# Two decoder layers on one core: projections in column pairs by seven products, attention on plain fp32, and every engine in a planned order

## The chip, the cores and the metric

The kernel runs on one core of a Trainium2 chip. The core has five engines: TensorE (PE: matmuls and transposes, results in eight PSUM banks of 512 columns), VectorE (DVE), ScalarE (ACT), GpSimd (POOL) and SyncE (SP), whose queue issues all DMAs here. Each engine runs its own instructions in order and waits for the others by semaphores. The metric is the device time of one execution in microseconds; less is better.

## The reference

Two layers on x (1024 rows by 1024 columns), all in fp32:

```python
for l in range(DEPTH):                                   # 2
    ada = c_act @ w_ada[l] + b_ada[l]
    shift, scale, gate = jnp.split(ada, 3, axis=-1)
    h = rmsnorm(x, norm_g[l]) * (1.0 + scale[:, None, :]) + shift[:, None, :]
    p = h @ w_in[l]                                      # 1024 x 9224
    mq, mk, mv, mo, mz, mi, mf, rq, rk, rv, rz = split_cols(p)
    qk = jax.nn.silu(causal_dwconv(jnp.concatenate([mq, mk], axis=-1), conv_w[l], conv_b[l]))
    ...
    cell = mlstm_chunkwise(mq_c, mk_c, mv, mi + b_igate[l], mf + b_fgate[l])     # 4 heads x 256
    y_m = jax.nn.sigmoid(mo) * head_layernorm(cell, gn_m[l], N_HEADS_MLSTM) * jax.nn.silu(mz)
    ret = retention_chunkwise(rq_h, rk_h, rv)                                    # 4 heads x 256, rotary q, k
    y_r = head_layernorm(ret, gn_r[l], N_HEADS_RET) * jax.nn.silu(rz)
    y = jnp.concatenate([y_m, y_r], axis=-1) @ w_out[l]  # 2048 x 1024
    x = x + gate[:, None, :] * y
return rmsnorm(x, final_g)
```

Each head is causal and works chunk by chunk: scores of q and k under a mask of decays, times v, plus q times a state of 256 x 256 that each chunk updates (mLSTM has a further column for the normaliser), then a norm over the head's 256 columns.

## The kernel before, in words

**Number format.** TensorE takes its fast fp32r form of each operand, so every fp32 tile is split in two: a rounded part hi and the rest lo. `split_to` (L620) casts hi on ACT (L621) and subtracts on GpSimd or VectorE to get lo (L622). A product is `mm3` (L144 to L147): hi by hi, hi by lo, lo by hi.

**Projections.** The normalised x is kept transposed (`hT`, eight k tiles of 128 rows, two halves of 512 positions, hi and lo). A block is 128 columns of `w_in`: two loads of 256 KB (`load_w_raw`, L338), two splits into wH and wL, and `proj_units` (L363) with 8 k x 2 halves x 3 matmuls of 512 columns into a PSUM bank (`pp`). v is projected the other way round, positions on partitions, in `v_path` (L579): 8 row tiles x 8 k x 3 matmuls of 256 columns, so that its result has the layout that attention wants. Per layer there are 72 blocks and 8 gate columns: at first z and o of head 0 and a second z block (made k by k while the norm comes in, in layer 0 by a script string with the steps S, Q, N, K, T, H, F ... written out by hand, L1200 to L1281), then v of head 0 with the gate columns, then head after head: 0 to 3 mLSTM (q and k with a convolution over four positions, `qk_ml` with `conv_silu`, L630 to L644; v, z, o), 4 to 7 retention (q and k with rotary, `qk_ret`, L701 to L717; v, z).

**Attention.** `attention` (L743) works in four chunks of 256 rows, launched as a generator whose pieces run between pieces of the projections. Operands are split: scores from q and k in hi and lo (L145 to L147, and `diagonal`), state updates by L772 and `mm3`, values from the state (cH, cL, L855) and from the scores (sH, sL, L845 and `mm3`). q, k in columns and v come directly from the projections' PSUM banks. k is also needed by rows: it is transposed in blocks of 32 on VectorE, stored to a DRAM tile `kdr` (L653) and gathered back (L663, four DMAs a chunk with runs of 64 elements). Normalised results go out to `ndr` (L919), gates to `gdr` (L553); the output projection loads both, multiplies them (L972, L976), splits the product, and makes `out_units` (L985).

**Order.** TensorE's order is the one written by hand: what `run_units`, `launch` and `tick` (L120 to L142) emit. The other engines are ordered by the framework's scheduler. At the start a few matmuls on a constant (step D of the script, L1263) keep TensorE busy ahead of the first products. The sums of w_ada times silu(c), which give scale and shift, run on VectorE (L246, L266) and are summed over partitions by TensorE (L251).

Of the kernel before, what the change touches and what calls it, by code (L numbers as in the profile page):

```python
# [19 lines left out]
P = 128  # L20
# [58 lines left out]

@with_exitstack  # L80
def tile_hybrid_trunk(ctx, tc, x, xt, c, positions, w_ada, b_ada, norm_g, w_in, conv_w, conv_b,
                      b_igate, b_fgate, gn_m, gn_r, w_out, final_g, consts, out):
    nc = tc.nc
    V, A, G, PE, Q = nc.vector, nc.scalar, nc.gpsimd, nc.tensor, nc.sync

# [4 lines left out]
    big = ctx.enter_context(tc.tile_pool(name="big", bufs=62))  # L90
    wrk = ctx.enter_context(tc.tile_pool(name="wrk", bufs=2))
    dpool = ctx.enter_context(tc.tile_pool(name="dram", bufs=1, space=DRAM))
    pp = ctx.enter_context(tc.tile_pool(name="pp", bufs=4, space=PSUM))
    pa = ctx.enter_context(tc.tile_pool(name="pa", bufs=4, space=PSUM))
# [3 lines left out]
    def nm(s):  # L98
        uid[0] += 1
        return f"{s}_{uid[0]}"  # L100

    def bt(dt=F32, n=512):
        return big.tile([P, n], dt, tag="b", name=nm("b"))

    def wt(tag, n, bufs, dt=F32):
        return wrk.tile([P, n], dt, tag=tag, bufs=bufs, name=nm(tag))

    def ps_a():
        return pa.tile([P, 512], F32, tag="a", name=nm("pa"))

    def ps_p():
        return pp.tile([P, 512], F32, tag="p", name=nm("pp"))

    def f(ap):
        return ap.bitcast(F32)

    clock = [0]
    pending = []

    def launch(gen, delay=0):  # L120
        uid[0] += 1
        pending.append([clock[0] + delay, uid[0], gen])

    def tick():
        clock[0] += 1
        while True:
            due = [p for p in pending if p[0] <= clock[0]]
            if not due:
                return
            p = min(due, key=lambda q: (q[0], q[1]))  # L130
            try:
                p[0] = clock[0] + next(p[2])
            except StopIteration:
                pending.remove(p)

    def drain():
        while pending:
            tick()

    def run_units(gen):  # L140
        for _ in gen:
            tick()  # L142

    def mm3(o, lt, rt, start, stop):  # L144
        PE.matmul(o, lt[0], rt[0], start=start, stop=False)  # L145
        PE.matmul(o, lt[0], rt[1], start=False, stop=False)  # L146
        PE.matmul(o, lt[1], rt[0], start=False, stop=stop)  # L147

    ident = cst.tile([P, P], F32, tag="ident", name="ident")
    make_identity(nc, ident)  # L150
    ones = cst.tile([P, 1], F32, tag="ones", name="ones")
    V.memset(ones, 1.0)
    mhalf = cst.tile([P, 4], F32, tag="mhalf", name="mhalf")
    V.memset(mhalf, -0.5)
    rmask = cst.tile([P, 384], F32, tag="rmask", name="rmask")
    V.memset(rmask, 1.0)
    ones_r = cst.tile([P, P], F32R, tag="ones_r", name="ones_r")
    V.tensor_copy(ones_r, rmask[:, 0:P])
    G.affine_select(rmask[:, 0:256], rmask[:, 0:256], [[1, 256]], ALU.is_ge, 0.0, base=0, channel_multiplier=-1)
    G.affine_select(rmask[:, 256:384], rmask[:, 256:384], [[1, 128]], ALU.is_ge, 0.0, base=0, channel_multiplier=-1)  # L160
    kc = cst.tile([P, N_CONST], F32, tag="kc", name="kc")
    Q.dma_start(kc, consts)

    xdr = [dpool.tile([D, HALF], F32, name=f"xdr{i}") for i in range(2)]
    ndr = [[[dpool.tile([8, 32, HALF], F32, name=f"ndr{l}_{h}_{i}") for i in range(2)] for h in range(8)]
           for l in range(DEPTH)]
    gdr = [[[[dpool.tile([P, HALF], F32, name=f"gdr{l}_{h}_{m}_{i}") for i in range(2)] for m in range(2)]
            for h in range(8)] for l in range(DEPTH)]
    kdr = [[[dpool.tile([HD, HALF], F32, name=f"kdr{l}_{h}_{i}") for i in range(2)] for h in range(8)]
           for l in range(DEPTH)]  # L170
    mdr = [dpool.tile([NH, T], F32, name=f"mdr{l}") for l in range(DEPTH)]

    cols = [None, None]
    gsh = [cst.tile([P, 2, KT], F32, tag=f"gsh{l}", name=f"gsh{l}") for l in range(DEPTH)]

    def load_ada_rows(l):
        rows = wt("rows", P, 2)
        Q.dma_start(rows[0:8, :], norm_g[l].rearrange("(r c) -> r c", c=P))
        Q.dma_start(rows[8:32, :], b_ada[l].rearrange("(r c) -> r c", c=P))
        return rows  # L180

    def load_head_rows(l):
        rows = wt("rows", P, 2)
# [4 lines left out]
        bg = cst.tile([P, 1], F32, tag=f"bg{l}", name=f"bg{l}")  # L188
        Q.dma_start(bg[0:4, :], b_fgate[l].unsqueeze(1))
        Q.dma_start(bg[32:36, :], b_igate[l].unsqueeze(1))  # L190
        return rows, bg

    def ada_cols(l, rows):
        cl = cst.tile([P, P], F32, tag=f"cols{l}", name=f"cols{l}")
        bg = None
        pt = ps_a()
        PE.transpose(pt[:, 0:32], rows[0:32, :], ident[0:32, 0:32])
        V.tensor_copy(cl[:, 0:8], pt[:, 0:8])
        V.tensor_copy(cl[:, 104:128], pt[:, 8:32])
        cols[l] = (cl, bg)  # L200

    def head_cols(l, rb):
        rows, bg = rb
        cl = cols[l][0]
        pt = ps_a()
        PE.transpose(pt[:, 0:96], rows[0:96, :], ident[0:96, 0:96])
        V.tensor_copy(cl[:, 8:88], pt[:, 0:80])
        V.tensor_scalar(cl[:, 88:96], pt[:, 80:88], 0.25, None, ALU.mult)
        V.tensor_scalar(cl[:, 96:104], pt[:, 88:96], 0.5, None, ALU.mult)
        cols[l] = (cl, bg)  # L210

    def gn_col(l, h, ct):
        return cols[l][0][:, 88 + 2 * h + ct:89 + 2 * h + ct]

    cact = cst.tile([P, KT], F32, tag="cact", name="cact")
    cth = cst.tile([P, KT], F32, tag="cth", name="cth")

    def load_cact(crow):
        pt = ps_a()
        PE.transpose(pt[:, 0:8], crow[0:8, :], ident[0:8, 0:8])  # L220
        A.activation(cth, pt[:, 0:8], AF.Tanh, scale=0.5)
        V.scalar_tensor_tensor(cact, cth, 1.0, pt[:, 0:8], ALU.add, ALU.mult)
        V.tensor_scalar(cact, cact, 0.5, None, ALU.mult)

    def finish_gsh(l, k, n, psh, psc):
        cl = cols[l][0]
        V.tensor_tensor(gsh[l][:, 1, k:k + n], psh, cl[:, 104 + k:104 + k + n], ALU.add)
        t1 = wt("sm1", 4, 2)[:, 0:n]
        V.scalar_tensor_tensor(t1, psc, 1.0, cl[:, 112 + k:112 + k + n], ALU.add, ALU.add)
        V.tensor_tensor(gsh[l][:, 0, k:k + n], t1, cl[:, k:k + n], ALU.mult)  # L230

    def ada_load(l, g):
        raws = []
        for kk in range(KT):
            raw = bt()
            Q.dma_start(raw.rearrange("p (w c) -> p w c", w=2),
                        w_ada[l, kk * P:(kk + 1) * P].rearrange("p (w c) -> p w c", c=D)[:, 0:2, g * 256:(g + 1) * 256])
            raws.append(raw)
        return raws

    def ada_group(raws, acc, kks):
        for kk in kks:
            if kk == 0:
                V.tensor_scalar(acc, raws[0], cact[:, 0:1], None, ALU.mult)
            else:
                V.scalar_tensor_tensor(acc, raws[kk], cact[:, kk:kk + 1], acc, ALU.mult, ALU.add)  # L246

    def ada_sums(l, g, acc, pt):
        for which in range(2):
            for i in range(2):  # L250
                PE.matmul(pt[:, 4 * g + 2 * which + i:4 * g + 2 * which + i + 1],  # L251
                          acc[:, which * 256 + i * P:which * 256 + (i + 1) * P], ones, start=True, stop=True)

    def ada_rows(l, c0, accs):
        acc = bt()
        accs.append(acc)
        prev = None
        for k in range(KT + 1):
            raw = None
            if k < KT:  # L260
                raw = wt("raw", 512, 4)
                Q.dma_start(raw, w_ada[l, k * P:(k + 1) * P, c0:c0 + 512])
            if k == 1:
                V.tensor_scalar(acc, prev, cact[:, 0:1], None, ALU.mult)
            elif k > 1:
                V.scalar_tensor_tensor(acc, prev, cact[:, k - 1:k], acc, ALU.mult, ALU.add)  # L266
            prev = raw
            yield 2

    def ada_columns_later(l):  # L270
        for half in range(2):
            accs = []
            for which in range(2):
                yield from ada_rows(l, which * D + half * 512, accs)
            yield 2
            pt = ps_a()
            for which in range(2):
                for i in range(4):
                    PE.matmul(pt[:, which * 4 + i:which * 4 + i + 1], accs[which][:, i * P:(i + 1) * P], ones,
                              start=True, stop=True)  # L280
# [1122 lines left out]
```

## Time and profile before

| What | Before |
|---|---|
| time of the runs, median of 3 | 2299.13 us (2298.86 to 2301.01) |
| span of the profiled execution | 2298.7 us |
| instructions | 34322 |
| TensorE busy | 2269.4 us, 99% |
| VectorE busy | 1338.7 us, 58% |
| ScalarE busy | 926.5 us, 40% |
| GpSimd busy | 827.5 us, 36% |
| SP's DMA queue | 359932 packets, 257.00 MB, 39.8% of 16 DMA engines' span |
| mean granted TensorE clock | 0.999 |

How to read it: a busy time is the sum over an engine's instructions, each from its start to its end, overlaps counted once. Rows of the profile name line, engine, operation, out<-in tiles and shapes, then a count; "busy, mean ns" and the idle time just ahead of them, with what ended it, stand at the end. A timeline row has start and length in front and "xN" for N like instructions in a row. PE's ends are modelled (the page's mean of a 512-column matmul is 395 ns), so the distance between two starts tells more than a length. The profiled execution's time is its span; what lies around the span is not recorded, and the span is 0.4 us below the median of the runs.

### The profile page before, as it was taken

To read this page: it belongs to the slowest core of one execution; us is meant where nothing else is said; L and a number is where in the kernel's file an instruction comes from. 1 tells how busy PE (TensorE), PEld (TensorE's weight loads), DVE (VectorE), ACT (ScalarE), POOL (GpSimd) and SP (SyncE) were. 2 spreads that over 40 slices of the span, in tenths; PEclk is the share of its full clock that TensorE was granted. 3 is DMA by queue.
4 is the path that set the end of the run, shared out by engine and by line. 5 is a ranking of instruction groups with operands and counts; after the bars stand their busy time and mean duration, and the time that the engine had idled before them with its cause. 6 is when DMAs were issued, how large, how long until landed. Compare 5 with 4: busy or idle time off the path is not lost. (4 is left out here: it accounts for less than half of the span.)

```text
span 2298.7 us, 34322 instructions
## 1 busy us (share of the span) xinstructions
PE 2269.4 (99%) x12411; PEld 1953.7 (85%) x12411; DVE 1338.7 (58%) x2821; ACT 926.5 (40%) x1785; POOL 827.5 (36%) x820
## 2 busy tenths in 40 slices
PE   7999999999999999999999999999999999999998
PEld 5888888889988888988888889888898898988886
DVE  7467688556555555585435676555564545556563
ACT  7535433444332323343544454444343323234442
POOL 0343333333333334224562434333334334341313
PEclk9999999999999999999999999999999999999999
DMA  8333333324433533476532323233223233436674
GB/s 258 80 69 94 83 80 82 83 70 115 124 110 87 149 96 79 126 254 212 169 105 67 84 71 82 77 77 79 68 71 98 74 91 88 124 84 205 184 242 125
DMA packets 360246, 259.45 MB, mean 113 GB/s; under 512 B 113266, under 2 KB 297338, under 8 KB 360076
## 3 DMA queue, kind: packets, MB, share of 16 engines
q1 hardware_dynamic: 359932, 257.00, 39.8%
q8 instruction: 97, 1.59, 0.3%
q14 instruction: 73, 0.60, 0.1%
q10 hardware_dynamic: 144, 0.26, 0.0%
HBM read 201.57 MB, written 55.61 MB: 112 GB/s over the span
## 5 line engine op out<-in xcount | busy, mean ns | idle before, releaser
L145 PE MATMUL pp<-b,wH 128*128 128x512 f32 x1824 | 719.6, 395 | 0.0
L146 PE MATMUL pp<-b,wH 128*128 128x512 f32 x1824 | 718.6, 394 | 0.0
L147 PE MATMUL pp<-b,wL 128*128 128x512 f32 x1824 | 717.6, 393 | 0.0
L622 POOL TENSOR_TENSOR wL<-raw,wH 128x512 fp32r<-128x512 f32 x338 | 453.9, 1351 | 542.3 <-ACT wH L621 478.7
L147 PEld LDWEIGHTS pp<-b,wL 128*128 128x128 f32 x1824 | 342.5, 188 | 80.4
L145 PEld LDWEIGHTS pp<-b,wH 128*128 128x128 f32 x1824 | 342.7, 188 | 73.1 <-DVE g L550 0.3
L146 PEld LDWEIGHTS pp<-b,wH 128*128 128x128 f32 x1824 | 342.5, 188 | 72.1 <-issue 0.2
L621 ACT CAST wH<-raw 128x512 fp32r<-128x512 f32 x402 | 245.7, 616 | 310.8 <-PE pp L146 109.9
L145 PE MATMUL pp<-wH,b 128*128 128x256 f32 (+1 forms) x1024 | 303.0, 296 | 0.0
L147 PE MATMUL pp<-wH,b 128*128 128x256 f32 (+1 forms) x1024 | 301.9, 295 | 0.0
L146 PE MATMUL pp<-wL,b 128*128 128x256 f32 (+1 forms) x1024 | 301.9, 295 | 0.0
L622 POOL TENSOR_TENSOR b<-acc,b 128x256 fp32r<-128x256 f32 (+1 forms) x192 | 176.6, 939 | 299.0 <-ACT b L621 287.7
L146 PEld LDWEIGHTS pp<-wL,b 128*128 128x128 f32 x1024 | 192.9, 188 | 5.8
L145 PEld LDWEIGHTS pp<-wH,b 128*128 128x128 f32 x1024 | 192.4, 188 | 6.0 <-DVE g L550 0.3
L147 PEld LDWEIGHTS pp<-wH,b 128*128 128x128 f32 x1024 | 192.7, 188 | 5.7
L639 DVE SCALAR_TENSOR_TENSOR acc<-pp,cols,acc 128x511 f32<-128x511 f32 (+2 forms) x192 | 142.4, 742 | 40.7 <-ACT acc L634 38.8
L621 ACT CAST b<-acc 128x256 fp32r<-128x256 f32 (+1 forms) x192 | 83.8, 476 | 180.7 <-DVE acc L716 129.3
L622 POOL TENSOR_TENSOR sL<-th,sH 128x256 fp32r<-128x256 f32 (+1 forms) x62 | 57.9, 934 | 207.7 <-ACT sH L621 161.9
L643 ACT ACTIVATE th<-acc 128x512 f32<-128x512 f32 x64 | 40.5, 632 | 145.7 <-DVE acc L641 77.9
L621 ACT CAST cH<-cf 128x516 fp32r<-128x516 f32 (+1 forms) x80 | 49.8, 622 | 105.8 <-DVE va L903 55.7
L622 DVE TENSOR_TENSOR wL<-raw,wH 128x512 fp32r<-128x512 f32 x64 | 44.3, 694 | 62.5 <-ACT wH L621 58.7
L145 PE MATMUL pa<-b,b 128*128 128x256 f32 (+1 forms) x256 | 72.3, 283 | 1.8 <-DVE th L787 1.0
(297 smaller groups left out, 3639.2 us busy)
## 6 DMA issues: line engine op xcount, KB each, us to landing
raw<-in_w_in_dram SPq DMA_DIRECT2D x274, 256.0 KB
raw<-in_w_out_dram SPq DMA_DIRECT2D x128, 256.0 KB
gdr<-g SPq DMA_DIRECT2D x64, 256.0 KB
ndr<-zt SPq DMA_DIRECT2D x128, 128.0 KB
raw<-in_w_ada_dram SPq DMA_DIRECT2D x64, 256.0 KB
g<-gdr SPq DMA_DIRECT2D x64, 256.0 KB
acc<-ndr SPq DMA_DIRECT2D x64, 256.0 KB
acc<-kdr SPq DMA_DIRECT2D x192, 64.0 KB
```

The source lines that it names most:

```text
L145: PE.matmul(o, lt[0], rt[0], start=start, stop=False)
L146: PE.matmul(o, lt[0], rt[1], start=False, stop=False)
L147: PE.matmul(o, lt[1], rt[0], start=False, stop=stop)
L621: A.copy(dst[0], src)
L622: eng.tensor_tensor(dst[1], src, f(dst[0]), ALU.subtract)
L639: V.scalar_tensor_tensor(acc[:, d:], pt[:, 0:HALF - d], wcol, acc[:, d:], ALU.mult, ALU.add)
L643: A.activation(th, acc, AF.Tanh, scale=0.5)
```

## The change

**The program is recorded, then planned.** Every instruction is first recorded as an `Op` with its tiles (`Program.record`), with names of tiles as `x`, `araw`, `raw`, `wH`. `Program.order` then simulates list scheduling with a duration for each operation (`cost`: 0.005 + 0.000443 n us for a split matmul of n columns, 0.004 + 0.00167 n for plain fp32, 0.185 + 0.00105 n on VectorE, 0.22 + 0.00084 n on ACT, 0.07 for a DMA's issue, a total rate of 185 KB per us), four rounds, and gives the order of all five engines and the slot of each tile. All instructions are then issued in that order from one line, L1720.

**Pairs.** 34 pairs of column blocks a layer replace the plain blocks, apart from z and o of head 0; v of head 0 and the gate columns stay as they were. A pair is cut in two column blocks x two halves of k x two halves of the positions, and made by seven products of 4 k x 3 matmuls in place of eight. The sums of hT that this needs are made once a layer (`sums_of_input`: 16 subtractions on VectorE and 16 splits); four sums of weights, seven splits, four copies from PSUM and three additions from PSUM come for each pair. One product of a pair is carried over into the next one (`finish_pair`). The subtraction for wL is on VectorE.

```diff
-    def proj_units(w, hT, evac):
-        for half in range(2):
-            pt = ps_p()
-            for k0 in (0, 4):
-                half_block(pt, w, hT, half, k0, k0 + 4)
...
-    def split_to(dst, src, eng=G):
+    def split_to(dst, src, eng=None):
         A.copy(dst[0], src)
-        eng.tensor_tensor(dst[1], src, f(dst[0]), ALU.subtract)
+        (eng or V).tensor_tensor(dst[1], src, f(dst[0]), ALU.subtract)
...
+    def product(pt, w, form, first, last):
+        for k in range(4):
+            cs = slice(k * P, (k + 1) * P)
+            mm3(pt, (w[0][:, cs], w[1][:, cs]), forms[form][k], first and k == 0, last and k == 3, skip_group_check=True)
...
+    def pair(c1, c2, lead, done1, done2, last=False):
+        a11, a21, a22 = block(c1, 0), block(c2, 0), block(c2, 1)
+        s1 = new("raw", 512, "s1", slots=raw_slots())
+        pX, pW = bank("p"), None
+        product(pX, split(a11), "B11", True, True)
+        a = new("c", 512, "ca")
+        A.copy(a, pX)
+        V.tensor_tensor(s1, a21, a22, ALU.add)
+        pW = bank("p")
+        product(pW, split(s1), "T1", True, True)
+        c = new("c", 512, "cc")
+        A.copy(c, pW)
+        finish_pair()
+        V.tensor_tensor(a21, a21, a11, ALU.subtract)
+        V.tensor_tensor(a11, s1, a11, ALU.subtract)
+        product(pX, split(a11), "T2", False, True)
+        b = new("c", 512, "cb")
+        A.copy(b, pX)
+        a12 = block(c1, 1)
+        pZ = bank("p")
+        product(pZ, split(a12), "B21", True, True)
+        x1 = new("X", W_X, "x")
...
+        V.tensor_tensor(h1[0], pZ, a, ALU.add)
+        V.tensor_tensor(a12, a12, a11, ALU.subtract)
+        w4 = split(a12)
+        w3 = split(a21)
...
+            product(pW, w4, "B22", False, True)
+            V.tensor_tensor(h1[1], pW, b, ALU.add)
...
+            product(pX, w3, "T3", False, True)
+            V.tensor_tensor(h2[1], pX, c, ALU.add)
```

**Attention.** Its matmuls take plain fp32 tiles, one for each product. v is now projected like every other block, transposed in blocks of 32 on VectorE, and stored; q, k, v all go out to DRAM (`qdr`, `kdr`, `vdr`, `v0dr`) and come back by chunk: `load_qk` (four loads), `gather` for v and for k by rows (eight DMAs of 32x4x64 each). States are kept as `cf` alone.

```diff
-            for part in range(2):
-                for dt in range(2):
-                    qq = qT[dt][j]
-                    for i in range(2 - part):
-                        PE.matmul(pi[:, 0:W], qq[:, i * CH + tt * P:i * CH + (tt + 1) * P],
-                                  state[part][:, dt, 0:W], start=part + dt + i == 0,
-                                  stop=ml and part + dt == 2)
+            for dt in range(2):
+                PE.matmul(pi[:, 0:W], qs[j][:, dt, tt * P:(tt + 1) * P], state[:, dt, 0:W].part(dt),
+                          start=dt == 0, stop=ml and dt == 1)
...
+        def load_qk(j):
+            for which, res, cls in ((0, qs, "q"), (1, ks, "kk")):
+                t = new(cls, 512, cls).rearrange("p (m t) -> p m t", m=2)
+                for m in range(2):
+                    Q.dma_start(t[:, m, :].part(m), qdr[hg][which][m][:, j * CH:(j + 1) * CH])
+                res[j] = t
...
+        def gather(src, j, a):
+            s = new("st", 512, "st")
+            for m in range(2):
+                for tb in range(4):
+                    o = tb * a * 32 + j * 64
+                    Q.dma_start(s[tb * 32:(tb + 1) * 32, m * 256:(m + 1) * 256].rearrange("i (b c) -> i b c", c=64)
+                                .part((m, tb)), src[m].rearrange("(b i) t -> i b t", i=32)[:, :, o:o + 64])
+            return s.rearrange("p (b t c) -> p t b c", t=2, c=32)
```

**The start.** The script string and its matmuls on a constant are gone; the planner orders the norm and the first columns too. On SP, before, the small rows and the first half of x stand first (`rows_235` is c, `rows_237` norm_g and b_ada, `b_240` to `b_247` x):

```order
L162 DMA kc<-in_consts_dram 128x17
L1159 DMA rows_235<-in_c_dram 8x128
L178 DMA rows_237<-in_norm_g_dram 8x128
L179 DMA rows_237<-in_b_ada_dram 24x128
L1148 DMA b_240<-in_x_dram 128x512
L1148 DMA b_241<-in_x_dram 128x512
```

After, SP's first rows are the constants, c and 18 tiles `araw` of w_ada, of which the last two stand here, ahead of the first half of x:

```order
L1720 DMA araw_145<-in_w_ada_dram 128x2x256
L1720 DMA araw_148<-in_w_ada_dram 128x2x256
L1720 DMA x_151<-in_x_dram 128x512
L1720 DMA x_155<-in_x_dram 128x512
L1720 DMA x_158<-in_x_dram 128x512
```

Six more `araw` and the second half of x follow, and then the rows of norm_g and b_ada (`rows_247`):

```order
L1720 DMA x_239<-in_x_dram 128x512
L1720 DMA x_243<-in_x_dram 128x512
L1720 DMA rows_247<-in_norm_g_dram 8x128
L1720 DMA rows_247<-in_b_ada_dram 24x128
L1720 DMA araw_250<-in_w_ada_dram 128x2x256
```

So x moved behind w_ada and the small rows behind all of x. TensorE's first rows after, where `aacc` are sums of w_ada and `x_158` is a tile of x, put the transpose of `rows_247` ahead of those of x:

```order
L1720 MATMUL pa_98<-ident_86,crow_74 128x8
L1720 MATMUL pa_139<-ones_88,aacc_107 128x1 x4
L1720 MATMUL pa_139<-ones_88,aacc_129 128x1 x4
L1720 MATMUL pa_272<-ident_86,rows_247 128x32
L1720 MATMUL pa_274<-ident_86,x_158 128x128
```

Before, `rows_237` came right behind c, and then the matmuls on a constant (`rmask`) and x:

```order
L220 MATMUL pa_366<-ident,rows_235 128x8
L197 MATMUL pa_372<-ident,rows_237 128x32
L1263 MATMUL pp_400<-b_256,rmask 128x256 x2
L327 MATMUL pa_411<-ident,b_240 128x128
L327 MATMUL pa_411<-ident,b_242 128x128
```

The transposes of x follow as before; the row that they stand behind now comes late in SP's queue.

**Loads of attention.** On SP before, at a retention head: gates (`gdr`), k out (`kdr`), k back in rows (`acc`), and weights:

```order
L653 DMA kdr_6_0_199<-th_9106 128x512
L653 DMA kdr_6_0_199<-th_9113 128x512
L663 DMA acc_9119<-kdr_6_0_199 32x8x64 x4
L663 DMA acc_9124<-kdr_6_0_199 32x8x64 x4
L653 DMA kdr_6_1_200<-th_9164 128x256
```

After, in the middle of layer 0, q (`q`), k (`kk`), the gathers (`st`) and weights (`raw`) share it:

```order
L1720 DMA st_7284<-kdr_5167 32x4x64 x4
L1720 DMA st_7284<-kdr_5110 32x4x64 x4
L1720 DMA qdr_7318<-x_7143 128x1024
L1720 DMA kk_7333<-qdr_5157 128x256
L1720 DMA kk_7333<-qdr_5079 128x256
L1720 DMA st_7339<-vdr_4323 32x4x64
L1720 DMA raw_7341<-in_w_in_dram 128x4x128
L1720 DMA st_7339<-vdr_4323 32x4x64 x3
L1720 DMA st_7339<-vdr_4531 32x4x64 x4
L1720 DMA raw_7355<-in_w_in_dram 128x4x128
```

One chunk's v alone is eight rows' worth of DMAs, between which a weight tile now stands.

**Splits.** GpSimd before, in a stretch of projections with attention beside them (`sL` and `dm` belong to attention):

```order
L622 TENSOR_TENSOR wL_3546<-raw_3543,wH_3545 128x512
L622 TENSOR_TENSOR wL_3552<-raw_3549,wH_3551 128x512
L622 TENSOR_TENSOR sL_3252<-th_3237,sH_3251 128x384
L763 AFFINE_SELECT dm_3255<-dm_3255 128x128 x2
L622 TENSOR_TENSOR sL_3286<-th_3274,sH_3285 128x256
```

VectorE after, in a stretch of pairs: sums of weights (`s_673`, and `raw` in place), lo parts (`wL`), and the rest:

```order
L1720 TENSOR_TENSOR s_673_1846<-raw_1751,raw_1797 128x512
L1720 TENSOR_TENSOR raw_1751<-raw_1751,raw_1745 128x512
L1720 TENSOR_TENSOR rt_1580<-rt_1580,rt_1756 128x256
L1720 TENSOR_TENSOR wL_1861<-raw_1745,wH_1851 128x512
L1720 TENSOR_TENSOR raw_1745<-s_673_1846,raw_1745 128x512
L1720 STREAM_TRANSPOSE vt_1870<-x_1779 128x8x4x32
L1720 TENSOR_TENSOR wL_1883<-s_673_1846,wH_1874 128x512
```

The subtractions moved from GpSimd's queue into VectorE's. In all, TensorE has 8781 instructions where it had 12356, SP 2291 DMAs where it had 1321, GpSimd 228 instructions where it had 822.

More of the change, by code (lines that the diff above doesn't have):

```diff
@@ L136, in drain @@
[L136 to L151, printed above, removed]
+        slots = classes[cls] if slots is None else slots
@@ L212, in gn_col @@
[L212 to L223, printed above, removed]
+        V.tensor_copy(cl[:, 8:88].part("h"), pt[:, 0:80])
@@ L238, in ada_load @@
             raws.append(raw)
[L239 to L252, printed above, removed]
```

2150 lines of the change are left out of this document (1210 added, 940 removed), and 8 rows, old and new, of the table script.

## The prediction

> **What bounds the kernel now.** I read the page first, then TensorE's busy time in three windows, then the start row by row, then single prices.
>
> ```profile
> span 2298.7 us, 34322 instructions
> ...
> PE 2269.4 (99%) x12411; PEld 1953.7 (85%) x12411; DVE 1338.7 (58%) x2821; ACT 926.5 (40%) x1785; POOL 827.5 (36%) x820
> ...
> PE   7999999999999999999999999999999999999998
> ...
> L622 POOL TENSOR_TENSOR wL<-raw,wH 128x512 fp32r<-128x512 f32 x338 | 453.9, 1351 | 542.3 <-ACT wH L621 478.7
> ```
>
> ```profile
> 0.00:24.00 24.00, 10.50 (x45) 8.42 (x45) 11.37 (x30) 14.49 (x32) 2.53 (x9) 1.00 0.89 294
> ...
> 0.00:70.00 70.00, 53.16 (x254) 42.16 (x255) 45.09 (x98) 50.58 (x101) 12.34 (x25) 1.00 0.72 226
> 70.00:2280.00 2210.00, 2205.02 (x12112) 1902.76 (x12111) 1284.45 (x2708) 870.17 (x1673) 813.04 (x792) 1.00 0.39 109
> 2280.00:2298.70 18.70, 11.24 (x49) 8.80 (x47) 9.13 (x16) 5.79 (x12) 2.16 (x4) 0.89 0.29 112
> ```
>
> The first number after a window's length is TensorE's busy time. It misses 16.8 us in the first 70, 5.0 in the next 2210 and 7.5 at the end: 29.3 in all. So the time is the sum of the matmuls, each at the distance from its start to the next one's, and a change is worth the matmul time that it removes, less the new idle time of TensorE. The sums are made against the span, 2298.7; the median of the runs, 2299.13, lies 0.4 above it, and I add that at the end.
>
> **The products.** Distances first: the first and the last rows of two unbroken stretches, and three rows around a product on plain fp32.
>
> ```profile
> 923.36 0.40 PE L145 MATMUL pp<-b,wH 128*128 128x512 f32 x1
> ...
> 937.28 0.28 PE L145 MATMUL pp<-wH,b 128*128 128x256 f32 x1
> ...
> 942.23 0.28 PE L145 MATMUL pp<-wH,b 128*128 128x256 f32 x1
> ```
>
> ```profile
> 1097.32 1.02 PE L1096 MATMUL pa<-g,ones_r 128*128 128x512 f32 x2
> 1097.77 0.80 PE L145 MATMUL pp<-b,wH 128*128 128x512 f32 x1
> 1098.41 0.39 PE L146 MATMUL pp<-b,wH 128*128 128x512 f32 x1
> ```
>
> From 923.36 to 937.28 stand 60 split products of 512 columns: 0.232 us each. From 937.28 to 942.23 stand 42 of 256: 0.118. The L1096 product is one matmul on plain fp32, which runs as two instructions: from 1097.32 to 1098.41 less the one split product between leaves 0.858, so 0.43 for 256 columns, and 0.215 for 128 if that halves again. Set against three split products of 256 (0.354) plain fp32 is dearer, against four cheaper.
>
> Projections before: 56 blocks a layer of 8 k, two halves and three matmuls, so 2 x 56 x 48 = 5376 of 512, and v of seven heads, 2 x 7 x 192 = 2688 of 256: 1247.2 + 317.2 = 1564.4 us. After, the order holds 34 pairs a layer (not 35), each 7 x 4 x 3 = 84 matmuls of 512, and two plain blocks a layer: 5712 + 192 = 5904, so 1369.7. That removes **194.7**. One eighth is saved of the pairs alone: v of head 0 and the output projection keep their products.
>
> ```profile
> L772 PE MATMUL pa<-b,b 128*128 128x256 f32 x384 | 55.9, 281 | 0.4 <-ACT n L908 0.4
> ...
> L845 PE MATMUL pa<-b,sL 128*128 128x258 f32 x24 | 4.4, 292 | 0.3
> ```
>
> ```profile
> L855 PE MATMUL pa<-cH,b 128*128 128x258 f32 x192 | 31.0, 284 | 0.4 <-ACT cH L621 0.4
> ```
>
> Attention before has 2208 such products (scores by L145 to L147, updates by L772, values by L845 and L855): 2208 x 0.118 = 260.5. After, 608 on plain fp32 of 256 or 258 columns and 192 of 128: 608 x 0.43 + 192 x 0.215 = 302.7, which adds **42.2**. The 128-column ones stand in no row; between half of the 256-column price and all of it they cost 41 to 83, and I take the half, since 512 columns are linear against 256 in the split rows (0.232 to 0.118). The warm-up matmuls (L1263, 14 instructions) go: **3** less. TensorE's work falls by 155.5.
>
> **The start.** DMAs on SP:
>
> ```profile
> 2.32 3.67 SPq L1148 DMA_DIRECT2D b<-in_x_dram  x8
> 6.03 6.02 SPq L236 DMA_DIRECT2D b<-in_w_ada_dram  x8
> ...
> 14.89 5.56 SPq L1148 DMA_DIRECT2D b<-in_x_dram  x8
> ```
>
> ```profile
> 12.55 2.04 PE L1263 MATMUL pp<-b,rmask 128*128 128x256 f32 x4 [8.71 <-DMA b<-in_w_ada_dram]
> 15.02 6.99 PE L327 MATMUL pa<-ident,b 128*128 128x128 f32 x32 [0.42 <-ACT b L320]
> 21.85 1.03 PE L1263 MATMUL pp<-b,rmask 128*128 128x256 f32 x4
> ...
> 26.13 0.50 PE L1200 MATMUL pp<-b,wH 128*128 128x512 f32 x1
> ```
>
> Before, x comes first, TensorE transposes it at 15.02 and makes the first product at 26.13. After, 18 tiles of w_ada are queued ahead of x, then 6 more, and the small rows of norm_g and b_ada come behind both halves of x, 40 tiles of 256 KB down the queue. At 294 GB/s (window 0:24) that is 10.5 MB, or 35.7 us. Their transpose stands in TensorE's order ahead of all transposes of x, so these start at about 36 and not at 15, take the same 7, and ten rows of VectorE at 0.6 stand before the first product: about 49 and not 26, so +23. Behind it stand some 22 us of products for half 0 (48 of 512 columns, 96 of 264), which wait for the scales of the later column groups now and then, as before: I put the idle time gained at **+25**. Bounds: +15 if the queue runs at 377 GB/s, the 8 tiles in 5.56 us of the third SP row (27.8 us for the 40 tiles, 8 less), and nothing waits behind; +37 if each of three later groups costs 4 us.
>
> [...]
>
> **VectorE, GpSimd, ACT.** The subtraction that makes wL moves from GpSimd to VectorE, and each pair adds four weight sums and three additions from PSUM.
>
> ```profile
> L622 DVE TENSOR_TENSOR wL<-raw,wH 128x512 fp32r<-128x512 f32 x64 | 44.3, 694 | 62.5 <-ACT wH L621 58.7 <-PE pa L146 2.1 <-DMA g<-gdr 1.5
> ...
> L716 DVE TENSOR_TENSOR acc<-acc,th 128x512 f32<-128x512 f32 x32 | 28.9, 903 | 0.0
> ...
> L717 DVE TENSOR_TENSOR acc<-acc,th 128x512 f32<-128x512 f32 x32 | 22.9, 716 | 0.0
> ```
>
> ```profile
> L639 DVE SCALAR_TENSOR_TENSOR acc<-pp,cols,acc 128x511 f32<-128x511 f32 x64 | 47.6, 744 | 38.8 <-ACT acc L634 38.8
> ```
>
> A pair has 14 such VectorE operations at 0.69: 9.7 us beside 84 x 0.232 = 19.5 of TensorE. An mLSTM head (five pairs and its attention, 97.4 + 18.9 = 116 of TensorE) needs 48 for its pairs, 16 convolution steps of 1024 columns at twice L639's 0.74, so 24, and, by some 40 further rows of the order at 0.7, 28 for gates, transposes, statistics and states: 100. So VectorE stays under TensorE, and I cost it at nothing; if that cover goes, see below. ACT, 40% busy before, gets 272 PSUM copies and loses the casts of q, k, v and states; hidden too.
>
> **SP and the attention's operands.** q and v now go through DRAM as k did: SP's DMAs rise from 1321 to 2291.
>
> ```profile
> L663 SPq DMA_DIRECT2D acc<-kdr x192: 302/448/1644, 170.6 to 2071.6; - x192
> ```
>
> The middle number is the median of an issue, 0.448 us. 2291 at about 0.4 are 917 us of 2180, 42%; a chunk's 20 loads (4 of q and k, 8 each of v and k) take 9 us, and a head has 36 us of them in about 100 of TensorE. Where the order packs them (about 40 us of TensorE's work in layer 0 ask for 56 of SP's issue) TensorE waits up to 16; where the first scores of a retention head follow its first gather, some 2 us a head, part of it taken up by the order's own spacing. I take **+10**; at least 0, at most 40, twice that one dense place and 1 us for each of 8 heads. SP's queue also holds the weights, so a gather that waits holds back the next raw tile.
>
> **Sum.** 2298.7 - 194.7 + 42.2 - 3.0 + 25 + 10 = 2178.2; with 0.4 for the median, 2179. With the bounds of the start and of SP alone this case runs from 2159 to 2221; the low end I put at 2150, since part of the 5 us of idle time in the middle may also go.
>
> **Rivals.** *Gathers lie open (slower).* TensorE's order is fixed, so a score whose q or k isn't there stops all projections behind it. A head's first two chunks are 40 DMAs, 18 us of issue, and start when its v and k have been stored. The point that decides is the gain without the +10, 2299 - 2169 = 130 us, over 16 heads: 8.1 a head. If 10 of the 18 lie open, +160 takes the place of the +10: 2329. For it: every load of a head waits in one queue behind weights, and the L663 row reaches 1.6 us. Against it: before, k took the same way and L772's row shows 0.4 us of idle time in all; and the order leaves room between: in layer 0 the first scores come after 20 of the 34 pairs.
> *VectorE becomes the bound.* L716 and L717 are the same operation on the same shape, 903 and 716 ns: 1.26 times. If such a price held for all of an mLSTM head, its 100 us would be 126 against 116: 10 for each of 8 heads, 80 in all, so 2259. Against: what runs beside VectorE is mostly GpSimd's 454 us of L622, and these are removed. [...]
> *Half of the first rival*, 3 to 7 us a head: 2217 to 2281.
> *Nothing gained*, 7.8 to 8.4 us a head: 2294 to 2304. That the products aren't fewer is no rival, since the order counts them.
>
> **How the numbers follow.** A measurement of this kernel tells about 0.2% from no change, 4.6 us. Chances: the forecast 0.71; VectorE 0.09; half-open gathers 0.08; within 0.2% 0.03; open gathers 0.09. So faster 0.88, same 0.03, slower 0.09. The range takes the forecast's case, 2150 to 2221, and reaches on to 2260, over VectorE's case and the nearer half of half-open gathers; beyond it lie fewer than 2 in 10.
>
> **What would show it.** TensorE's busy time about 2114 at the same clock, with idle time near 65: about 42 in the first 70 us, about 8 at the end, and some 15 in between, put down to DMAs of q, k or v. The plain products should stand 0.43 apart, and L622's GpSimd row should be gone, with VectorE's busy time up by some hundred us and still under TensorE's. It is wrong if the idle time in the middle is over 40 with VectorE or ACT as releaser, if idle gaps stand at each head's first scores, or if the 512-column distance isn't 0.232.

## The result, and the profile after

| | Before | After | Forecast |
|---|---|---|---|
| median of the runs | 2299.13 us | 2314.66 us (2313.45 to 2316.14, 3 runs) | 2179 (2150 to 2260) |
| ratio, 95% interval | | 1.0066 [1.0046, 1.0086] | 0.948 |
| span of the profiled execution | 2298.7 us | 2311.7 us | |

The changed kernel is 0.7% slower, where 5% faster was forecast. The page of after, in the rows that answer to those of before:

```profile
span 2311.7 us, 30256 instructions
...
PE 2161.7 (94%) x9629; PEld 1764.6 (76%) x9629; DVE 1690.6 (73%) x3054; ACT 1065.1 (46%) x1938; POOL 189.4 (8%) x223
...
PE   3899999999999999997897999999989999999998
...
q1 hardware_dynamic: 490252, 359.04, 53.4%
...
L1720 POOL TENSOR_TENSOR oL<-wo,oH 128x512 fp32r<-128x512 f32 x64 | 83.6, 1307 | 211.0 <-ACT oH L1720 206.6
```

TensorE has 107.7 us less busy time, but it is idle for 150.0 us of the span and not for 29.3. GpSimd's 454 us of wL are gone. Where the idle time lies, by stretches (the first number behind the length is TensorE's busy time, the last one GB/s):

```profile
0.00:70.00 70.00, 28.80 (x127) 22.59 (x127) 54.88 (x121) 29.15 (x67) 12.09 (x14) 0.93 0.72 222
...
600.00:1000.00 400.00, 376.20 (x1680) 309.34 (x1679) 283.23 (x596) 176.73 (x358) 25.22 (x43) 0.97 0.63 176
1000.00:1150.00 150.00, 127.60 (x537) 101.67 (x535) 78.08 (x118) 52.71 (x89) 30.43 (x24) 0.93 0.67 218
1150.00:1300.00 150.00, 130.61 (x638) 108.63 (x639) 98.17 (x180) 80.45 (x136) 16.86 (x16) 0.91 0.29 83
1300.00:2100.00 800.00, 785.82 (x3489) 644.72 (x3488) 614.88 (x1091) 387.96 (x712) 36.17 (x60) 0.99 0.52 149
2100.00:2312.00 212.00, 192.13 (x803) 150.81 (x801) 103.28 (x166) 75.21 (x142) 50.13 (x43) 0.96 0.69 198
```

The start misses 41.2 us, about what was forecast. But 600 to 1000 (attention of layer 0) misses 23.8, the change of layers from 1000 to 1300 misses 41.8, and the end from 2100 misses 19.6 up to the span's end. TensorE's own waits say for what:

```profile
PE pa L1720 <- DVE aacc L1720: 26.7, 4, 13.0
PE pa L1720 <- DVE g L1720: 16.0, 2, 12.3
PE pp L1720 <- DVE hf L1720: 15.7, 1, 15.7
PE pa L1720 <- DMA q<-qdr: 11.3, 6, 4.8
PE pp L1720 <- ACT aH L1720: 8.6, 2, 4.8
PE pp L1720 <- ACT oH L1720: 7.9, 4, 3.8
PE pa L1720 <- DVE dg L1720: 6.9, 1, 6.9
```

`aacc` is the start. The rest is spread over many releasers, and the DVE rows don't mean that VectorE is the bound: from 1000 to 1150 it is busy 78 of 150 us. The 15.7 us for `hf` show what stands behind such a row. Here are TensorE's timeline, SP's and VectorE's (`hf` there is the residual x by columns, which VectorE adds to a PSUM bank of the output projection; TensorE's next product needs that bank):

```profile
1081.97 0.39 PE L1720 MATMUL pp<-yH,oL 128*128 128x512 f32 x1
1098.03 0.80 PE L1720 MATMUL pp<-yH,oH 128*128 128x512 f32 x1 [15.66 <-DVE hf L1720]
1098.62 0.63 PE L1720 MATMUL pp<-yL,oH 128*128 128x512 f32 x1
1099.05 0.63 PE L1720 MATMUL pp<-yH,oL 128*128 128x512 f32 x1
...
1101.61 0.44 PE L1720 MATMUL pp<-yH,oL 128*128 128x512 f32 x1
1101.89 0.39 PE L1720 MATMUL pp<-yH,oH 128*128 128x512 f32 x1
```

```profile
555.86 1.51 SPq L1720 DMA_DIRECT2D st<-vdr  x3
...
1084.37 0.32 SPq L1720 DMA_DIRECT2D yr<-ndr  x1
1088.31 0.33 SPq L1720 DMA_DIRECT2D hf<-in_xt_dram  x1
1090.11 0.32 SPq L1720 DMA_DIRECT2D yr<-ndr  x1
...
1092.66 0.38 SPq L1720 DMA_DIRECT2D hf<-in_xt_dram  x1
```

```profile
1095.08 0.69 DVE L1720 TENSOR_TENSOR yg<-yr,yg 128x512 f32<-128x512 f32 x1 [0.65 <-DMA yg<-gdr]
...
1097.23 0.75 DVE L1720 SCALAR_TENSOR_TENSOR hf<-pp,gcol,hf 128x512 f32<-128x512 f32 x1
```

TensorE stops at 1082.4. The first of four late loads of `hf` is issued at 1088.31, between loads of the next half's results (`yr`), which wait for free slots (2.4 us in four waits for VectorE's `yg` from 1082 to 1097.5); SP's issues stand in the planned order, the `hf` of 1092.66 0.41 us behind a `yr`, so the residual waits with them. On VectorE too the addition that ends the wait stands behind a row on the next half's results, which waited for a load of its own. The order on SP and VectorE, not an engine's speed, made this wait.

To sum it up I took every matmul's distance to the next one. The usual distance of its shape counts as work; what goes beyond it is a wait where the trace records idle time or the distance is over two and a half times the usual one; the rest is "slow". In the rows above the distance is 0.43 from 1098.62 to 1101.61, where the granted clock is 0.50, and 0.23 after it.

| us of TensorE | work | waits | of them in 0:100, 100:1000, 1000:1300, later | slow |
|---|---|---|---|---|
| before | 2253.8 | 24.7 | 17.5, 3.6, 0.8, 2.9 | 9.6 |
| after | 2099.8 | 158.7 | 43.4, 38.7, 44.5, 31.8 | 41.6 |

With 3 us ahead of the first matmul and 8 from the last one's start to the end these are the spans, to within 1 us. Work fell by 154.0, as forecast (155.5). Waits took back 134.0, slow matmuls 32.0.

### The profile page after: what moved, and what is told of

It is laid out like the page before. It is cut to its first block, busy times and chain, and to the rows that moved or that the text cites. A ratio compares the mean times of both kernels' runs of the same rounds, so it can differ in the third digit from the quotient of the medians.

```text
span 2311.7 us, 30256 instructions
## 1 busy us (share of the span) xinstructions
PE 2161.7 (94%) x9629; PEld 1764.6 (76%) x9629; DVE 1690.6 (73%) x3054; ACT 1065.1 (46%) x1938; POOL 189.4 (8%) x223
## 3 DMA queue, kind: packets, MB, share of 16 engines
q1 hardware_dynamic: 490252, 359.04, 53.4%
## 5 line engine op out<-in xcount | busy, mean ns | idle before, releaser
L1720 PE MATMUL pp<-hL,wH 128*128 128x512 f32 x1968 | 789.1, 401 | 3.3 <-DVE hL L1720 2.3
L1720 PE MATMUL pp<-hH,wH 128*128 128x512 f32 x1968 | 788.9, 401 | 1.9 <-ACT wH L1720 1.2
L1720 PE MATMUL pp<-hH,wL 128*128 128x512 f32 x1968 | 786.7, 400 | 1.5 <-DVE wL L1720 1.2
L1720 ACT CAST wH<-raw 128x512 fp32r<-128x512 f32 x416 | 256.5, 619 | 437.7 <-PE pp L1720 316.3
L1720 PEld LDWEIGHTS pp<-hL,wH 128*128 128x128 f32 x1968 | 372.2, 189 | 88.9 <-DVE hL L1720 2.9
L1720 PEld LDWEIGHTS pp<-hH,wL 128*128 128x128 f32 x1968 | 372.0, 189 | 88.2 <-DVE wL L1720 4.2
L1720 PEld LDWEIGHTS pp<-hH,wH 128*128 128x128 f32 x1968 | 372.2, 189 | 85.8 <-ACT wH L1720 1.6
L1720 DVE TENSOR_TENSOR wL<-raw,wH 128x512 fp32r<-128x512 f32 x416 | 285.8, 689 | 113.3 <-ACT wH L1720 108.0
L1720 POOL TENSOR_TENSOR rsd<-va,mhalf 128x2 f32<-128x2 f32 x64 | 48.2, 753 | 1190.0 <-DVE va L1720 1054.2
L1720 ACT CAST oH<-wo 128x512 fp32r<-128x512 f32 x128 | 77.8, 616 | 138.8 <-PE pa L1720 64.2
L1720 DVE SCALAR_TENSOR_TENSOR acc<-x,cols,acc 128x1024 f32<-128x1024 f32 x96 | 122.7, 1278 | 1.9 <-ACT acc L1720 1.6
L1720 PE MATMUL pa<-cf,q 128*128 128x258 f32 (+1 forms) x384 | 109.4, 393 | 7.2 <-DVE cf L1720 6.8
L1720 PE MATMUL pa<-v,kt 128*128 128x258 f32 (+1 forms) x384 | 101.6, 388 | 0.1
L1720 POOL TENSOR_TENSOR oL<-wo,oH 128x512 fp32r<-128x512 f32 x64 | 83.6, 1307 | 211.0 <-ACT oH L1720 206.6
L1720 PEld LDWEIGHTS pa<-q,kk 128*128 128x128 f32 x512 | 77.2, 194 | 28.7 <-DMA q<-qdr 9.2
L1720 PE MATMUL pa<-q,kk 128*128 128x128 f32 (+1 forms) x512 | 84.8, 309 | 14.7 <-DMA q<-qdr 11.3
L1720 PE MATMUL pa<-v,sd 128*128 128x258 f32 (+1 forms) x320 | 90.0, 388 | 6.9 <-ACT v L1720 6.4
L1720 DVE TENSOR_TENSOR raw<-raw,raw 128x512 f32<-128x512 f32 x136 | 93.7, 689 | 3.2
L1720 PEld LDWEIGHTS pa<-cf,q 128*128 128x128 f32 x384 | 71.5, 195 | 23.2 <-DVE cf L1720 9.3
L1720 ACT ACTIVATE nr<-nd,nmu,rsd 128x256 f32<-128x256 f32 x128 | 71.4, 594 | 37.6 <-DVE nmu L1720 28.2
L1720 DVE SCALAR_TENSOR_TENSOR yL<-yg,cols,yH 128x512 fp32r<-128x512 f32 x64 | 52.2, 816 | 47.7 <-ACT yH L1720 47.3
L1720 PEld LDWEIGHTS pa<-v,kt 128*128 128x128 f32 x384 | 74.5, 195 | 13.1 <-ACT nd L1720 0.8
```

Of the source, the lines that this page charges most:

```text
L1720: getattr(engines[op.eng], op.fn)(*[real(v) for v in op.a], **{n: real(v) for n, v in op.k.items()})
```

## The experiments

**The theories.** The planner prices a DMA at 0.07 us of SP's time and all transfers together at 185 KB/us. The traces say otherwise. Three gathers back to back take SP 1.51 us, 0.50 each (row above); 218 GB/s flow between 1000 and 1150, and before had 294 in its first 24 us. At 185 the kernel's 359.04 MB would be 1941 us of transfer, so the plan must space TensorE's work out wherever traffic is dense. *Theory A:* the waits are written into the order by these wrong prices, so another order of the same instructions (with other slots for the tiles, which the plan also gives) is fast. *Rivals:* the waits are the chip's whatever the order says, because SP's queue (theory C) or the late operands of attention (theory B) set the pace. All runs have the kernel before beside them on the same chip (2299.3 to 2300.4 us).

**Rate alone, to 330.**

```diff
-    RATE = 185e3
+    RATE = 330e3
```

> The changed kernel, with one number of the planner's costs changed: the total DMA rate from 185 to 330 KB per us (the profile of the change moves 247 GB/s in its first slice, and before moved 299 GB/s between 24 and 50 us). All instructions are the same, only their order differs. Theory A, the order: TensorE's idle time of about 115 us between 100 and 2300 us is written into the order, since the planner held back loads for a DMA queue slower than the chip's and laid rows that wait for them late; then half to all of it goes, with the cold matmuls behind the gaps: 2225, between 2195 and 2255. Theory B, the chip: the loads of attention and of the output phase wait for SP's issues and for buffers whatever the order says; an order that asks for more at once then waits as much or more: 2290 to 2340.

2399.13 us, 1.0434 [1.0416, 1.0451]: worse, which no theory had. Where TensorE waits in it:

```profile
PE pa L1720 <- DMA q<-qdr: 28.8, 16, 5.5
PE pa L1720 <- DVE sd L1720: 24.9, 8, 6.9
PE pa L1720 <- DVE cf L1720: 23.7, 13, 4.5
```

These are attention's operands: loads of q, masked scores (`sd`) and states (`cf`). It looks as if with fast transfers and issues at 0.07 the plan puts DMAs closer than SP can issue them; the next run tests that. A as I had put it (the rate alone) falls.

**Rate 330 and issue 0.40; issue 0.40 alone.**

```diff
-            op.bytes, op.dur = total, (0.95 if eng == "POOL" else 0.07)
+            op.bytes, op.dur = total, (0.95 if eng == "POOL" else 0.40)
```

> As the run with the rate at 330, and the planner's cost of one DMA issue on SP also from 0.07 to 0.40 us, near what the trace shows (0.33 to 0.45). Theory A: within 10 us of the run with the rate alone, since SP is busy under half of the time. Theory B in its form that SP's issues are what the order misses: at least 20 us faster than the rate alone.

2311.39 us, 1.0047 [1.0032, 1.0062]: 88 us come back by the issue's price, where A asked for under 10, so the order did miss SP's issues.

> The changed kernel with only the planner's cost of one DMA issue changed, from 0.07 to 0.40 us; the rate stays at 185. Theory A: nothing, 2300 to 2325, since the rate still binds the planned transfers. Theory B by SP's issues: 2230 to 2280.

2317.69 us, 1.0074 [1.0059, 1.0089]: at 185 the same price changes nothing, as A said.

**Rate 130, the wrong way.** One line, `RATE = 130e3`.

> The changed kernel with the planner's DMA rate at 130 in place of 185: the suspected cost made larger. Theory A: more idle time in the order, over 2380 with TensorE's idle time spread over all heads. Theory B: 2290 to 2340, since the chip's own rate and buffers didn't change.

2531.35 us, 1.1003 [1.0981, 1.1026]: with the same operations and only a slower rate in the plan the kernel takes 217 us more than the changed kernel. A number in the planner does become idle time.

**Both prices near what the traces show: rate 300, issue 0.50.** Only these two numbers differ from the changed kernel.

> Only the order again: planner's rate 300 and issue 0.50 us, which is what SP takes from one start to the next in the crowded stretches (0.474 the median of the gathers, 0.65 the mean of the weight tiles). Theory C, SP's queue: between 450 and 1000 us SP issues DMAs back to back, and attention's loads come as fast as SP can issue them; a better order can only place the wait: 2285 to 2320, within 25 us of the order with issue 0.40. Theory A, a wrong order alone: with the right cost the waits go, 2240 or less.

2235.60 us, 0.9720 [0.9704, 0.9737]: 79 us under the changed kernel by order alone, and 2.8% under before. Theories B and C fall as put: SP's queue holds the same DMAs, and TensorE's waits from 100 to 1000 go from 38.7 to 25.5 us, those behind 1300 from 31.8 to about 5. The largest that are left, and where SP now issues the residual:

```profile
PE pa L1720 <- DVE aacc L1720: 22.2, 3, 12.3
PE pa L1720 <- DVE g L1720: 19.6, 2, 12.2
PE pa L1720 <- DMA rows<-in_b_ada_dram: 7.1, 1, 7.1
PE pa L1720 <- DVE dg L1720: 5.3, 1, 5.3
PE pa L1720 <- DVE hf L1720: 5.0, 1, 5.0
```

```profile
994.98 1.37 SPq L1720 DMA_DIRECT2D hf<-in_xt_dram  x3
...
1021.98 1.38 SPq L1720 DMA_DIRECT2D hf<-in_xt_dram  x3
```

The wait of 15.7 for `hf` is gone (the one of 5.0 was in after too): 13 of its loads go out between 995 and 1024, ahead of most loads of results. q's 11.3 us are 0.8, and the waits for `oH` and `aH` are gone too.

**Which of the two prices?** Rate 330 with issue 0.50, and rate 185 with issue 0.50, one number each away from the last run.

> Order only: the changed kernel with a planned rate of 330 KB/us and 0.50 us per DMA that SP issues (the second run had 330 and 0.40 and took 2311.4, the fifth 300 and 0.50 and took 2235.6). Which of the two numbers made those 76 us? If it was the issue (0.50 is what the trace shows between two small gathers back to back, 0.40 still lets the queue fall behind), this one stands at 2225 to 2255. If it was the rate (330 lets the weight loads be placed later than they can come), it stands at 2285 to 2315.

2247.25 us, 0.9771 [0.9756, 0.9786]: at 330 it was the issue's price.

> Order only: the changed kernel with its own planned rate of 185 KB/us and 0.50 us per DMA that SP issues. At 330 KB/us the step from 0.40 to 0.50 took 64 us off (2311.4 to 2247.3), and at 185 the step from 0.07 to 0.40 took nothing off (2314.7 to 2317.7). If the issue's price is the only number that matters and 0.40 is just below the point from which SP keeps up, this one stands at 2235 to 2260 too. If 185 by itself writes waits into the order (transfers planned to come far later than they do), the dearer issue is added to it, and it stands at 2300 or above, the more so since the two together make SP's planned transfers the longest chain.

2316.65 us, 1.0075 [1.0058, 1.0092]: 185 by itself keeps the waits, whatever an issue costs. The eight orders of the same operations together (us):

| | issue 0.07 | 0.40 | 0.50 |
|---|---|---|---|
| rate 130 | 2531.4 | | |
| rate 185 | 2314.7 | 2317.7 | 2316.7 |
| rate 300 | | | 2235.6 |
| rate 330 | 2399.1 | 2311.4 | 2247.3 |

Neither price pays by itself: at 185 the plan's rate binds and the issue's price makes no difference; at 330 the issue's price decides, and the step from 0.40 to 0.50 alone is worth 64 us. Theory A holds with two prices, not with one.

**Fewer DMAs.** v and k are stored so that a gather is two DMAs and not eight (a store four and not one; SP's DMAs fall by 444). With the new prices, and with the old ones:

```diff
-                for tb in range(4):
-                    o = tb * a * 32 + j * 64
-                    Q.dma_start(s[tb * 32:(tb + 1) * 32, m * 256:(m + 1) * 256].rearrange("i (b c) -> i b c", c=64)
-                                .part((m, tb)), src[m].rearrange("(b i) t -> i b t", i=32)[:, :, o:o + 64])
+                Q.dma_start(s[:, m * 256:(m + 1) * 256].rearrange("p (b c) -> p b c", c=64).part(m),
+                            src[m].rearrange("p (b t) -> p b t", b=4)[:, :, j * 64:j * 64 + 64])
```

> The planner's costs as in the run with 300 and 0.50, and the copies of k and v in DRAM laid out so that a chunk's gather takes 2 DMAs in place of 8 (128x4x64 each, the same runs of 256 bytes and the same bytes) and a store takes 4 in place of 1: 1846 DMAs on SP and not 2290. Theory C: SP's queue is what attention waits for, 444 fewer issues at 0.5 us are 222 us of SP, about 60 in the crowded stretches: 2215 to 2260. Theory D, the latency of each chunk's chain (load, scale on ACT, products, statistics) and the DMA engines' own time on runs of 256 bytes: no change against the run with 300 and 0.50, within 15 us.

2226.19 us, 0.9683 [0.9669, 0.9698]: 9 us less, which both theories' ranges hold, so this run alone doesn't decide between them.

> The gathers in 2 DMAs, but with the planner's costs as the change had them (0.07 us, 185 KB per us), so that the order keeps the idle time that these costs write into it. If the loss is two things, idle time in the order at the layer's end and SP's queue in attention: 2270 to 2300, between the change and the run with both. If the order is no cause at all: as fast as the run with both.

2279.26 us, 0.9912 [0.9897, 0.9927], in the range of two losses, order and SP's queue. In the bad order fewer DMAs are worth 35 us (waits from 100 to 1000 fall from 38.7 to 22.0), in the good one 9 (25.5 to 15.0). At the change of layers 41.7 of 44.5 stay under the old prices.

**x ahead of w_ada.** On top of the last good one, the loads of the first half of x and of the rows of norm_g and b_ada go to the head of SP's queue.

```diff
+        prog.early.update(prog.ops[-8:])
...
-                op.late = late
+                op.late = late - (1e4 if op in self.early else 0.0)
```

> As the run with gathers in 2 DMAs and costs 300 and 0.50, and on SP the first half of x and the rows of norm_g and b_ada ahead of w_ada, as the kernel before had them. Theory of the start as predicted, that x and the rows come too late: first product 15 us earlier and the whole 10 to 20 us faster. Rival: the sums of w_ada bound the start anyway, 32 tiles through VectorE: under 6 us faster.

2220.12 us, 0.9654 [0.9640, 0.9669]: 6 us only, and the first product of 512 columns starts at 40.3 instead of 41.1, not 15 earlier. Waits in the first 100 us are 46.8 against 41.8, slow matmuls 9.9 against 13.6, so the start itself didn't gain; the 6 us came from 100 to 1000, where waits fall from 15.0 to 8.8. In the first 100 us most of the waiting is now put down to VectorE's `x` (16.6 us in eight waits) and not to `aacc` (21.7 before).

**A place of its own for the gate columns.** The wait for `g` (12.3 at 1252 and 3.7 at 104 in after) goes back to a MEMSET. Its slot is one of those that tiles `hf` of the input use as well (at a layer's start `hf` is the normalised input, not the residual), and in VectorE's order it stands directly behind sums that read such tiles:

```profile
1249.75 1.29 DVE L1720 TENSOR_TENSOR hf<-hf,hf 128x512 f32<-128x512 f32 x2
1251.05 0.30 DVE L1720 MEMSET g<- 128x288 f32 x1
```

In the next run the tile of the MEMSET keeps its own place, and the split weights have nine slots and not ten.

```diff
-H_TAGS = [f"H{i}" for i in range(10)]
+H_TAGS = [f"H{i}" for i in range(9)]
...
+    g8 = keep("g8", (P, 288))
...
-        g8 = new("gc", 288, "g8")
```

> The eighth run (2220.1) with one further edit: the tile of the gate columns, in a slot that the attention's tiles also use and that comes free only when the sums of the input are done, has a place of its own (and one of the ten slots of the split weights is given up for the room). In the eighth run TensorE waits 12.2 us at 1192 and 7.5 us at 104 for this tile. If those waits are what they look like, about 12 to 19 us go: 2200 to 2210. If the sums of the input themselves hold TensorE there, the same wait comes back under another name, and it stays at 2215 to 2222.

2199.09 us, 0.9561 [0.9546, 0.9575]: 21.0 off, just more than the two waits of that run (19.6). It is the best of all versions, 4.4% under before. Its largest waits and its middle:

```profile
PE pa L1723 <- DVE x L1723: 17.4, 8, 6.3
PE pa L1723 <- DMA rows<-in_b_ada_dram: 7.8, 1, 7.8
PE pa L1723 <- DVE dg L1723: 5.2, 1, 5.2
```

```profile
100.00:1000.00 900.00, 895.99 (x4074) 740.31 (x4073) 745.78 (x1380) 448.08 (x806) 50.88 (x76) 1.00 0.60 171
```

TensorE misses 4 us in 900; `g` is gone from the waits.

**The seven products undone in that version.**

```diff
+            for i in range(2):
+                pt = bank("p")
+                product(pt, w0, f"B1{i + 1}", True, False)
+                product(pt, w1, f"B2{i + 1}", False, True)
```

> The eleventh kernel with the seven products undone: each of the 35 column pairs of a layer by eight products on the plain halves of the input, without the sums of input and weights (no part of the result is left out). 70 products of 12 matmuls come back: 840 x 0.231 = 194 us of TensorE. If TensorE's work is the bound there and the seven products cost nothing else, it takes 194 us more than the eleventh: 2395 to 2405. If the sums (VectorE, ScalarE and the 24 slots of summed forms) are behind a good part of the waits that are left, part of the 194 us is not lost, and it stands at 2340 to 2380: then the seven products are worth less than their matmuls.

2384.28 us, 1.0363 [1.0346, 1.0381], 185.2 over the version with seven. The expectation counted 35 pairs; there are 34 a layer, so 816 matmuls come back and not 840, as the page counts too (10445 matmuls against 9629):

```profile
span 2383.6 us, 29798 instructions
...
PE 2314.9 (97%) x10445; PEld 1901.1 (80%) x10445; DVE 1258.9 (53%) x2310; ACT 933.1 (39%) x1700; POOL 182.8 (8%) x223
```

816 x 0.232 are 189.3, and TensorE's work in the trace grew by just that. With that count the first theory asks for 2388 and the measured 2384 is 4 below: in this order the sums that seven products need (VectorE 442 us more) cost TensorE some 4 us and no more.

## Why the prediction was wrong

**The products: right.** 154.0 us less work against 155.5, and the 512-column distance is 0.231. The price of 128-column plain fp32, for which no row stood, was taken at half: its 384 distances have a median of 0.112 for each of two instructions, 0.224 against 0.215, so that held. That the pairs are worth their matmuls is shown by undoing them: 185 of 189.3.

**The start: the number right, the reason only in part.** 24.4 us of TensorE's busy time are missing in the first 70 (53.16 before, 28.80 after) against +25. The transposes of x did start at 35.8 (forecast 36), but the first product came at 41.8 and not at 49, and the products stood in a row only from 53.8 on, so that the number came out is in part luck. I blamed x behind 24 tiles of w_ada. With x first the waits of the start only changed their name, from `aacc` to `x`, and with the slow matmuls they kept their sum (55.4 and 56.7). So it isn't the place of x in the queue. What TensorE needs there has to be loaded and worked on by VectorE either way, and the trace of after points to VectorE's work: it is busy 54.9 of the first 70 us, and loads of w_ada kept it idle for 3.2. No run separates the two.

**"SP and the attention's operands, +10": the step that failed.** It was the sum's only term for new idle time behind the start, with a bound of 40. Behind the first 100 us waits rose by 107.7 (115.0 against 7.3) and slow matmuls by 28. Three things were wrong in it:
- I took "the order's own spacing" as a help. It was the harm: the spacing is what the plan believes of DMAs, and in the order of a wrong plan TensorE stands waiting for things that another order has ready. Changing two prices took 79 us off.
- I priced SP's issue only where attention reads its operands. DMA waits on q, k and v came to 14.4 us (11.3 + 1.6 + 1.5); with the two waits put down to ACT's `v` (6.4), which scales what the gathers of v bring just before, it is 20.8, twice the +10 and inside its bounds. The larger part was where I had no term at all. At the change of layers, 1000 to 1300, waits are 44.5 us: `hf` in the output projection, where traffic goes over the planned rate (218 GB/s up to 1150), then `g` and others at 83 GB/s. From 2100 on, at 198 GB/s, the output projection waits again.
- A tile's slot is part of the order too. `g` waited 16.0 us for one in after (19.6 in the run ahead of the fix); the fix took 21.

**The clock.** The sum had no term for slow matmuls. The first 100 us had 4.1 us of them more than before; the rest of the 32 came later, where the sum had +10 in all. The mean granted clock is 0.974 in after and 0.999 before. Slow matmuls fell together with the waits: 41.6 us in after, 26.1 in the run with 300 and 0.50, 19.2 in the best one.

**The rivals.** The time fell between "nothing gained" and "gathers lie open", by neither mechanism: a head's first two chunks didn't lie open, since the 20.8 us above are 1.3 for each of 16 heads and not 10, so the nearness of the numbers is chance. VectorE as the bound falls too, since with the same work of VectorE 2199 is reached, at 77% of its time. What the prediction set against it, that GpSimd's L622 is removed, fits the traces: before, nine of the 32 operations of L716 and one of the 32 of L717 took 1.23 to 1.78 us, each with L622 running beside it, and the other 54 took 0.67 to 0.69 (19 of them with part of an L622 beside them); after, VectorE's operations of that shape on two `raw` tiles take 0.69 in the mean. And the prediction's own sign of error came true, idle time in the middle over 40 with VectorE and ACT as releasers; only what it would mean was missing.

**What is left of the forecast.** With the order, the gathers and the slot repaired the sum nearly holds: 2199.1 against 2179. From 100 on, waits and slow matmuls are some 37 us in that version; before had 12 there and the sum added 10, so 15 are left; some 3 more are the start's and 1.5 the work's.

## What to carry to other kernels

A kernel whose order is planned from durations is as fast as its durations are right, and two of them can be wrong in a way that hides each other: measure what an issue takes in its queue and what the transfers reach together, and correct both at once. Saved matmuls are a gain only if TensorE stays fed (here 154.0 us of work less came with 134.0 us of new waits), so a forecast of such a change needs a term for every stage in which the order was made anew, above all where layers meet and where traffic is densest. Where a wait's releaser is named as an engine that is itself half idle, look for the load or the slot that it waits for.

## What the hardware showed

Two waits of TensorE in after cost more than their length, and one of them wasn't long. Behind the 15.66 us above, seven matmuls stand 0.43 apart and not 0.23. The same came behind a wait of 1.45 us, and later than one would look:

```profile
1024.99 0.50 PE L1720 MATMUL pp<-yH,oH 128*128 128x512 f32 x1 [1.45 <-ACT oH L1720]
1025.33 0.40 PE L1720 MATMUL pp<-yL,oH 128*128 128x512 f32 x1
1025.88 0.50 PE L1720 MATMUL pp<-yH,oL 128*128 128x512 f32 x1
...
1026.77 0.63 PE L1720 MATMUL pp<-yH,oL 128*128 128x512 f32 x1
1027.20 0.63 PE L1720 MATMUL pp<-yH,oH 128*128 128x512 f32 x1
...
1029.76 0.50 PE L1720 MATMUL pp<-yH,oH 128*128 128x512 f32 x1
1030.10 0.39 PE L1720 MATMUL pp<-yL,oH 128*128 128x512 f32 x1
```

From 1026.77 to 1029.76 seven matmuls stand 0.43 apart, 1.8 us after the wait, and the granted clock there is 0.50. Both times 3.0 us pass at 0.43, behind the wait of 15.66 us as behind the one of 1.45 (with one distance of 0.55 after it). No run was made to show what makes the clock fall.

A load of 256 KB (`wo`, a tile of w_out) holds SP no longer than a gather of 32 KB (`st`), 0.46 us and 0.47:

```profile
973.06 3.75 SPq L1720 DMA_DIRECT2D st<-vdr  x8
976.85 1.39 SPq L1720 DMA_DIRECT2D wo<-in_w_out_dram  x3
```

Over the whole trace of after, where SP doesn't wait between two issues, their starts stand 0.474 us apart in the median, 0.474 behind gathers and 0.446 behind tiles of w_in (`raw`). So one price for both fits this queue; a mean from start to start, like the 0.65 that an expectation above gives for weight tiles, can have SP's waits for free slots in it (239.8 us in 111 waits for VectorE's `wL`, which frees those of `raw`).
